# Differential attention by pairs of heads: the products with the values alternate between the halves of the result

## The chip, the core and the metric

The kernel runs on one core of a Trainium2 chip. A core has TensorE (PE in the profile; PEld is its weight load), VectorE (DVE), ScalarE (ACT), GpSimd (POOL) and SyncE (SP), which take their own lists of instructions in order and wait for each other by semaphores, and 16 DMA engines. TensorE writes into PSUM, a small memory of 8 banks of 512 fp32 columns. The metric is the device time of one execution in microseconds; lower is better. The time before is 1351.88 us, the median of three runs (1351.8 to 1352.84).

## What is computed

One decoder layer over 1024 tokens of width 1024: RMSNorm, one wide input projection, three token mixers side by side (Mamba-2 SSD, differential attention, mLSTM), an output projection, a SwiGLU FFN, a gated per-layer input and a last RMSNorm. The change is in the differential attention. It has 4 heads of value width 64; each head makes two softmaxes and subtracts one from the other:

```python
def diff_attention(q, k, v, lam, lam_init, rel_bias, norm_w):
    ...
    for j in range(s_ // Q_BLOCK):
        ...
        sc = jnp.einsum('bqhmd,bkhmd->bhmqk', qb, kb).astype(jnp.float32) * scale
        ...
        sc = sc + jnp.transpose(bias, (2, 0, 1))[None, :, None].astype(jnp.float32)
        sc = jnp.where(dist >= 0, sc, -1e30)
        a = jax.nn.softmax(sc, axis=-1)
        attn = a[:, :, 0] - lam * a[:, :, 1]
        outs.append(jnp.einsum('bhqk,bkhe->bqhe', attn.astype(v.dtype), vb))
    o = jnp.concatenate(outs, axis=1)
    ...
```

## The kernel before

Tokens are on the free axis, features on partitions. The input projection is a stream of matmuls `pj` (in fp32 split into a high and a low part, three matmuls for one) that runs all through the attention: `fill(us)` lets that stream issue as much as `us` microseconds of TensorE's time by an estimate, in steps of three matmuls, and is called after every part of a head. Behind a finished half of a projection ScalarE copies it out (`cst`, `conv`), and VectorE does three steps of a short convolution on it (`conv<-cst`, L594).

The attention goes over two pairs of heads (`hp`), and in each over the eight blocks of 128 queries (`qb`), from the longest to the shortest in the first pair and back up in the second. For one block and one head (`head`, L647) the work is, for each of the two softmaxes `m`: score matmuls into a PSUM bank `sc`, a VectorE operation that adds the bias and takes the minimum (L675, `e<-sc,tb`, one per 512 keys), an exponential on ScalarE with its sum (L678). Then VectorE takes a reciprocal (`rr`, L686), scales it (L687) and combines the two (`e<-e,rr`, L688). TensorE transposes the result by blocks of 128 keys into PSUM (`tp`, L695), up to four blocks at a time, ScalarE copies them to SBUF (`aT`, L698), and TensorE multiplies them with the values (`pv`, L704): weights are 128x64 values of this head, 128 columns are moved, and the result is one half of the partitions of `pv`, the lower for the first head of the pair and the upper for the second. Each fp32 matmul of `pv` is two rows of the profile.

The order on TensorE is the order of the program (class `InOrder`, L84, makes every matmul follow the one before). `run_attention` (L710) sets it: step `u` takes head `u` through its transposes and products, and beside it makes the scores of head `u + 2`, of `u + 3` where the next heads are short (`AHEAD`, L568). The other engines are ordered by the scheduler, by priority: the convolution steps have a low one (`late(L1)`), the copies `aT` a high one.

Of the kernel before, what the change touches and what calls it, by code (L numbers as in the profile page):

```python
# [11 lines left out]
F32 = mybir.dt.float32  # L12
# [7 lines left out]
P = 128  # L20
S = 1024
D = 1024
NT = S // P
# [81 lines left out]
def trunk(ctx: ExitStack, tc: tile.TileContext, a, out):  # L105
    nc = tc.nc
    sync, act, dve, pool, pe = nc.sync, nc.scalar, nc.vector, nc.gpsimd, InOrder(tc, nc.tensor)
# [10 lines left out]
    def right(name, bufs=1):  # L118
        return tc.alloc_tile_pool(name=name, bufs=bufs, side="right", reuse_waits="tile")
# [4 lines left out]
    def psum(name, bufs):  # L124
        return tc.alloc_tile_pool(name=name, bufs=bufs, space=PSUM, reuse_waits="tile")


    ident = const.tile([P, P], F32, name="ident")
# [49 lines left out]
    zp = right("zp", 1)  # L178
    p1pre = right("p1pre", 1)
    dv = p1pre.tile([P, NT, 256], F32, name="dv")  # L180
# [57 lines left out]
    @contextmanager  # L238
    def late(n):

        tc.cur_priority += n
        yield
        tc.cur_priority -= n
# [124 lines left out]
    for t0 in (0, 256):  # L368
        c = slice(t0, t0 + 256)
# [32 lines left out]
    p1 = right("p1", 1)  # L402
    SCB = 3
    psa = psum("psa", 2)
# [37 lines left out]
    def fill(us):  # L442

        owed[0] += us
        while owed[0] > 0 and done[0] < len(jobs):
            step()
# [118 lines left out]


    LATE = 600
    AHEAD = 3  # L568
    AW = 5
    L1, L2, L3 = 200, 0, -100  # L570
    R, F = (34, 42), (2.5, 0.8, 8.0)
# [25 lines left out]
    ym = [ymp.tile([P, 4, H2], F32, tag="ym", name=f"ym{i}") for i in range(2)]  # L597
# [5 lines left out]
    def attention(hp):  # L603

        tb = p1.tile([P, 1280], F32, tag="tb", name="tb", bufs=2)
        pool.memset(tb[:, 256:1024], 0.0)
        for hl, o in ((0, 1024), (1, 0)):  # L610
            sync.dma_start(tb[:, o:o + 256], skew[2 * hp + hl, 127:127 + P * 383]
                           .rearrange("(p u) -> p u", u=383)[:, 0:256])
            pool.affine_select(tb[:, o + P:o + 256], tb[:, o + P:o + 256], pattern=[[-1, P]],
                               compare_op=ALU.is_ge, fill=1e30, base=0, channel_multiplier=1)
        ks = {}

        def load_keys(i):
            ks[i] = p1.tile([P, 4, H2], F32R, tag="ks", name="ks", bufs=2)
            pool.dma_start(ks[i], k_d[hp][:, :, i * H2:(i + 1) * H2])

        for qb in (range(NT - 1, -1, -1) if hp == 0 else range(NT)):
            kl = (qb + 1) * P
            for i in ((0, 1) if qb >= 4 else (0,)):
                if i not in ks:
                    load_keys(i)
            q_ = p1.tile([P, 4, P], F32R, tag="qs", name="qs", bufs=2)
            pool.dma_start(q_, q_d[hp][:, :, qb * P:(qb + 1) * P])

            def col(hl, b, qb=qb):

                return b if hl == 0 or qb == 0 else (b - (qb - 1)) % (qb + 1)

            def runs(hl):

                o = []
                for b in range(qb + 1):
                    if o and col(hl, b) == o[-1][2] + o[-1][1] and col(hl, b) % 4 and b % 4:
                        o[-1][1] += 1
                    else:
                        o.append([b, 1, col(hl, b)])  # L640
                return o

            pv = [None]
            for hl in range(2):
                yield head(hp, qb, hl, q_, ks, tb, col, runs(hl), pv)

    def head(hp, qb, hl, q_, ks, tb, col, runs, pv):  # L647


        kl = (qb + 1) * P  # L650
        ks = dict(ks)
        e = []
        nm = p1.tile([P, 4], F32, tag="nm", name="nm", bufs=6)
        rs0 = asum[:, qb // 4, 4 * (qb % 4) + 2 * hp + hl:4 * (qb % 4) + 2 * hp + hl + 1]
        rs = p1.tile([P, 1], F32, tag="rs", name="rs", bufs=6)
        t_ = tb[:, 1280 - kl:1280] if hl == 0 else tb[:, 0:kl] if qb else tb[:, P:2 * P]
        for m in range(2):
            hm = 2 * hl + m
            if qb >= 4:
                em_ = p1.tile([P, S], F32, tag=f"e{m}", name="e", bufs=3 - m)  # L660
            elif m == 0:
                em_ = p1.tile([P, S], F32, tag=f"e{hl}", name="e", bufs=3 - hl)
            else:
                em_ = e[0][:, H2:]

            low = 3e38
            for c0 in range(0, qb + 1, 4):
                ps = psa.tile([P, H2], F32, tag="sc", name="sc", bufs=SCB)
                for b, n, c in runs:
                    if c // 4 == c0 // 4:  # L670
                        pe.matmul(ps[:, (c - c0) * P:(c - c0 + n) * P], q_[:, hm, :],
                                  ks[b // 4][:, hm, (b % 4) * P:(b % 4 + n) * P], start=True, stop=True)
                cc = slice(c0 * P, min(kl, (c0 + 4) * P))
                acc = nm[:, m + c0 // 2:m + c0 // 2 + 1]
                dve.tensor_tensor_reduce(em_[:, cc], ps[:, 0:cc.stop - cc.start], t_[:, cc], 1.0, low,  # L675
                                         ALU.add, ALU.min, acc)
                low = acc
            last_exp[0] = act.activation(em_[:, 0:kl], em_[:, 0:kl], AF.Exp, bias=low, scale=-1.0,  # L678
                                         accum_out=rs if m else rs0)
            e.append(em_)  # L680
            if m == 0:
                yield
        with late(L2):

            rr_ = p1.tile([P, 1], F32, tag="rr", name="rr", bufs=6)
            dve.reciprocal(rr_, rs)  # L686
            dve.scalar_tensor_tensor(rr_, rs0, rr_, nlam, ALU.mult, ALU.mult)  # L687
            dve.scalar_tensor_tensor(e[0][:, 0:kl], e[1][:, 0:kl], rr_, e[0][:, 0:kl], ALU.mult, ALU.add)  # L688
        yield
        for b0 in range(0, qb + 1, 4):  # L690
            n = min(4, qb + 1 - b0)
            tp = psa.tile([P, 4, P], F32, tag="pt", bufs=6 - SCB, name="tp")
            for b in range(n):
                c = col(hl, b0 + b) * P
                pe.transpose(tp[:, b, :], e[0][:, c:c + P], ident)  # L695
            t_ = zp.tile([P, 4, P], F32, tag="t2", name="aT", bufs=3)
            with late(L3):
                act.copy(t_[:, 0:n, :], tp[:, 0:n, :])  # L698
            yield
            if hl == 0 and b0 == 0:  # L700
                pv[0] = psa.tile([P, P], F32, tag="pt", bufs=6 - SCB, name="pv")
            h = 2 * hp + hl
            for b in range(n):
                pe.matmul(pv[0][hl * 64:(hl + 1) * 64, :], dv[:, b0 + b, h * 64:(h + 1) * 64], t_[:, b, :],  # L704
                          start=(b0 + b == 0), stop=(b0 + b == qb))
        if hl == 1:
            act.copy(ym[qb // 4][:, hp, (qb % 4) * P:(qb % 4 + 1) * P], pv[0])
        yield

    def run_attention():  # L710

        order = [(hp, qb) for hp in range(2) for qb in (range(NT - 1, -1, -1) if hp == 0 else range(NT))
                 for _ in range(2)]
        rate = [R[hp] / (4 * sum(qb + AW for qb in range(NT))) for hp in range(2)]
        src = (head_ for hp in range(2) for head_ in attention(hp))
        heads = []
        for u in range(-2, len(order)):

            small = u >= 0 and all(qb < 4 for _, qb in order[u:u + AHEAD + 1])
            new = []  # L720
            while len(heads) + len(new) <= min(u + (AHEAD if small else 2), len(order) - 1):
                new.append(next(src))
            heads += new
            us = rate[order[u][0]] * (order[u][1] + AW) if u >= 0 else F[0]
            for part in range(2):
                if u >= 0:
                    next(heads[u], None)
                for head_ in new:
                    next(head_)
                fill(us)  # L730
            if u >= 0:
                for _ in heads[u]:
                    pass

    jobs += [conv_job(4 + d, bcg, 4 + d, d) for d in range(4)]
    jobs += [conv_job(8 + d, xg, d, d) for d in range(4)]
    run_attention()
    finish(len(jobs))

# [378 lines left out]
    for half in range(2):  # L1118
# [5 lines left out]
        order = (0, 7, 1, 2, 3, 4, 5, 6)  # L1124
# [251 lines left out]
    for i in (1, 2, 5, 6, 7, 3, 4):  # L1376
        tag = "a" if i in (1, 6, 7, 4) else "b"
# [5 lines left out]
        for k in range(NP):  # L1383
            if k % 4 == 0:
                n = min(4, NP - k)
# [3 lines left out]
            t_ = unit(i, k, bs[:, k % 4], as_ and as_[:, k % 4])  # L1389
# [144 lines left out]
```

## Time and profile before

| what | value |
|---|---|
| median of three runs | 1351.88 us |
| profiled execution, its own time | 1353.48 us |
| its span in the profile | 1351.8 us |
| TensorE busy | 1307.7 us, 97% of the span |
| VectorE / ScalarE / GpSimd busy | 851.9 / 556.9 / 308.7 us |
| chain that ended last, on TensorE | 89% |
| attention: first score matmul to last product | 87 to 262 us |
| granted clock of TensorE, mean of the span / in 87 to 262 us | 0.988 / 1.00 |

Busy is the time in which an engine had an instruction under way; TensorE's overlap, and their ends are modelled, so 97% says only that it is rarely without work. The chain is followed back from the last instruction, at each step to what released it; a share of the chain is what shortening helps. The granted clock is a share of 2.4 GHz.

### The profile page before, as it was taken

What the parts mean: (1) busy time and instruction counts of PE and PEld (TensorE: products, weight loads), DVE (VectorE), ACT (ScalarE), POOL (GpSimd) and SP (SyncE); (2) the same over time, 40 slices, a digit from 0 to 9 for tenths busy, and PEclk for the clock granted to TensorE, in tenths of its full rate; (3) what the DMA queues carried; (4) which work ended last, traced back from release to release, by engine and by line L of the source; (5) the groups of instructions that cost most, each with busy time, mean ns of one, the idle gap of its engine ahead of it and who ended that gap; (6) DMA issues with size and microseconds to landing.
All of it is one profiled execution on the core that took longest, in us unless ns stands there. A gap on an engine that the chain in (4) does not pass through costs nothing.

```text
span 1351.8 us, 17848 instructions
## 1 busy us (share of the span) xinstructions
PE 1307.7 (97%) x6601; PEld 1067.6 (79%) x6601; DVE 851.9 (63%) x1619; ACT 556.9 (41%) x1101; POOL 308.7 (23%) x323
## 2 busy tenths in 40 slices
PE   6999999999999999979999999999979999999997
PEld 5977777777788888758888888888857888888897
DVE  7567778567656855588665564766536796576243
ACT  6346666643323533353333333333323444464121
POOL 4141322243334322242122111222210000000111
PEclk9999999999999999989999999999999999999999
DMA  6472341043312333013332232323389352223011
GB/s 210 164 227 79 80 100 48 19 127 102 91 51 64 104 133 110 32 62 118 117 117 91 96 107 73 114 105 117 120 308 367 112 175 92 80 72 116 8 63 63
DMA packets 66847, 149.84 MB, mean 111 GB/s; under 512 B 6116, under 2 KB 23304, under 8 KB 61640
## 3 DMA queue, kind: packets, MB, share of 16 engines
q1 hardware_dynamic: 52008, 129.82, 28.6%
q0 software_dynamic: 11872, 14.16, 3.9%
q10 hardware_dynamic: 2880, 4.72, 0.9%
q8 instruction: 52, 0.85, 0.3%
q14 instruction: 35, 0.29, 0.1%
HBM read 111.64 MB, written 37.82 MB: 111 GB/s over the span
## 4 chain that ended last, share of the span: by engine, by line
PE 89%; DVE 5%; DMA 3%; ACT 1%; issue 1%; POOL 1%; SPq 0%; POOLq 0%; DVEq 0%; ACTq 0%
PE pd L98 17%; PE a L98 17%; PE pj L98 16%; PE c L98 8%; PE po L98 7%; PE pg L98 6%; PE b L98 4%; PE pv L98 3%; PE pp L98 2%; PE tp L101 1%; PE sc L98 1%; PE py L98 1%; DMA ar<-in_w_down_dram 1%; PE pn L98 1%; PE pk L98 1%
## 5 line engine op out<-in xcount | busy, mean ns | idle before, releaser
L98 PE MATMUL pj<-uT,w 128*128 128x512 f32 x1056 | 276.6, 404 | 0.0
L98 PEld LDWEIGHTS pj<-uT,w 128*128 128x128 f32 x1056 | 192.5, 190 | 36.8 <-issue 0.3
L98 PE MATMUL pd<-un 128*128 128x512 f32 x924 | 212.4, 392 | 5.6 <-DVE un L140 4.7
L98 PEld LDWEIGHTS pd<-un 128*128 128x128 f32 x924 | 174.5, 189 | 43.5 <-DVE un L140 5.1
L140 POOL TENSOR_TENSOR w<-raw,w 128x256 fp32r<-128x256 f32 x88 | 78.6, 921 | 91.8 <-ACT w L139 91.5
L139 ACT CAST un<-ar 128x512 fp32r<-128x512 f32 x77 | 47.9, 622 | 121.4 <-PE pd L98 110.1
L98 PE MATMUL pg<-hT,wg 128*128 128x256 f32 (+1 forms) x576 | 94.0, 319 | 0.0
L98 PE MATMUL po<-yT,wo 128*128 128x512 f32 x384 | 89.8, 395 | 0.0
L98 PEld LDWEIGHTS pg<-hT,wg 128*128 128x128 f32 x576 | 82.7, 188 | 8.5
L98 PEld LDWEIGHTS po<-yT,wo 128*128 128x128 f32 x384 | 71.9, 188 | 16.6
L1500 POOL TENSOR_TENSOR ssq<-ssq,sq 128x256 f32<-128x256 f32 (+1 forms) x18 | 17.1, 952 | 291.2 <-ACT sq L1498 291.2
L140 DVE TENSOR_TENSOR un<-ar,un 128x512 fp32r<-128x512 f32 x77 | 53.0, 688 | 46.7 <-ACT un L139 46.4
L1243 ACT ACTIVATE c<-c 128x512 f32<-128x512 f32 x44 | 27.9, 633 | 98.4 <-DVE c L1242 98.4
L98 PE MATMUL c<-T1h,wX 128*128 128x512 f32 x176 | 59.9, 402 | 3.7 <-ACT wX L139 2.5
L678 ACT ACTIVATE e<-e,nm 128x1024 f32<-128x1024 f32 (+7 forms) x64 | 49.7, 777 | 32.8 <-DVE nm L675 32.5
L98 PE MATMUL a<-T2h,wY 128*128 128x512 f32 x176 | 60.9, 406 | 1.6 <-ACT T2h L139 1.6
L98 PE MATMUL a<-T4h,wV 128*128 128x512 f32 x176 | 60.1, 404 | 2.0 <-DVE c L1246 2.0
L98 PE MATMUL a<-T3h,wZ 128*128 128x512 f32 x176 | 59.1, 397 | 1.1 <-ACT c L1229 1.1
L140 POOL TENSOR_TENSOR wZ<-rgu,wZ 128x512 fp32r<-128x512 f32 x22 | 31.0, 1407 | 122.0 <-ACT wZ L139 110.3
L98 PE MATMUL b<-B21h,wY 128*128 128x512 f32 x176 | 58.6, 394 | 0.0
L98 PE MATMUL c<-B22h,wZ 128*128 128x512 f32 x176 | 58.3, 393 | 0.0
L98 PE MATMUL a<-B11h,wX 128*128 128x512 f32 x176 | 57.9, 390 | 0.0
(385 smaller groups left out, 2667.2 us busy)
## 6 DMA issues: line engine op xcount, KB each, us to landing
rgu<-in_w_gu_dram SPq DMA_DIRECT2D x22, 1024.0 KB, 4.9
opd<-c SPq DMA_DIRECT2D x77, 256.0 KB, 2.0
four<-opd SPq DMA_DIRECT2D x12, 1024.0 KB, 4.9
raw<-in_w_tiles_dram SPq DMA_DIRECT2D x22, 512.0 KB, 3.7
ar<-in_w_down_dram SPq DMA_DIRECT2D x11, 512.0 KB, 9.2
four<-opd SPq DMA_DIRECT2D x6, 768.0 KB, 4.2
xt<-in_x_dram SPq DMA_DIRECT2D x16, 256.0 KB, 4.6
q_d<-qk SPq DMA_DIRECT2D x16, 256.0 KB, 3.5
```

The source lines that it names most:

```text
L98: return self._behind(self.pe.matmul(*args, **kw))
L101: return self._behind(self.pe.transpose(*args, **kw))
L139: act.copy(hi, src)
L140: eng.tensor_tensor(lo, src, hi.bitcast(F32), ALU.subtract)
L678: last_exp[0] = act.activation(em_[:, 0:kl], em_[:, 0:kl], AF.Exp, bias=low, scale=-1.0, accum_out=rs if m else rs0)
L1243: act.activation(g, g, AF.Silu)
L1500: (dve if j == 7 else pool).tensor_tensor(ssq, ssq, sq, ALU.add)
```

## The change

`head` is split. `scores` (one head) ends behind the combination of its two softmaxes. `pair` makes the scores of both heads of a block of queries, and then goes over the keys two blocks at a time: four transposes, alternating between the two heads, into one PSUM tile, one copy `aT` of up to 512 columns, and four products `pv` that alternate between the lower and the upper half of the result. `run_attention` now goes by pairs: step `u` has four parts, and each takes pair `u` one chunk on and makes one part of the scores of pair `u + 1`. The fills of a pair are as many and as long as before. The weights `e` get four buffers for the first softmax and one for the second (three and two before).

```diff
-            pv = [None]
-            for hl in range(2):
-                yield head(hp, qb, hl, q_, ks, tb, col, runs(hl), pv)
+            yield pair(hp, qb, q_, dict(ks), tb, col, [runs(hl) for hl in range(2)])
+
+    def pair(hp, qb, q_, ks, tb, col, runs):
+        es_ = []
+        for hl in range(2):
+            e = []
+            yield from scores(hp, qb, hl, q_, ks, tb, runs[hl], e)
+            es_.append(e[0])
+        pv = None
+        for b0 in range(0, qb + 1, 2):
+            n = min(2, qb + 1 - b0)
+            tp = psa.tile([P, 2, 2, P], F32, tag="pt", bufs=6 - SCB, name="tp")
+            for b in range(n):
+                for hl in range(2):
+                    c = col(hl, b0 + b) * P
+                    pe.transpose(tp[:, b, hl, :], es_[hl][:, c:c + P], ident)
+            t_ = zp.tile([P, 2, 2, P], F32, tag="t2", name="aT", bufs=3)
+            with late(L3):
+                act.copy(t_[:, 0:n], tp[:, 0:n])
+            yield
...
+            for b in range(n):
+                for hl in range(2):
+                    h = 2 * hp + hl
+                    pe.matmul(pv[hl * 64:(hl + 1) * 64, :], dv[:, b0 + b, h * 64:(h + 1) * 64], t_[:, b, hl, :],
+                              start=(b0 + b == 0), stop=(b0 + b == qb))
...
-                em_ = p1.tile([P, S], F32, tag=f"e{m}", name="e", bufs=3 - m)
+                em_ = p1.tile([P, S], F32, tag=f"e{m}", name="e", bufs=4 - 3 * m)
...
-            for b in range(n):
-                pe.matmul(pv[0][hl * 64:(hl + 1) * 64, :], dv[:, b0 + b, h * 64:(h + 1) * 64], t_[:, b, :],
-                          start=(b0 + b == 0), stop=(b0 + b == qb))
...
-        for u in range(-2, len(order)):
-            small = u >= 0 and all(qb < 4 for _, qb in order[u:u + AHEAD + 1])
-            new = []
-            while len(heads) + len(new) <= min(u + (AHEAD if small else 2), len(order) - 1):
-                new.append(next(src))
-            heads += new
+        for u in range(-1, len(order)):
+            new = next(pairs, None)
             us = rate[order[u][0]] * (order[u][1] + AW) if u >= 0 else F[0]
-            for part in range(2):
+            for part in range(4):
                 if u >= 0:
-                    next(heads[u], None)
-                for head_ in new:
-                    next(head_)
+                    next(now, None)
+                if new:
+                    next(new)
                 fill(us)
```

On TensorE, where the first pair's block of 1024 keys ends and that of 896 keys begins, the order before was this. `e_1147` holds the weights of the new block's first head, and the `sc` row at the top is the last of its second head's scores.

```order
L98 MATMUL sc_1249<-ks_996,qs_1136 128x128
L98 MATMUL pj_1164<-uT101_91,w_1075 128x512
L98 MATMUL pj_1164<-uT111_93,w_1075 128x512
L98 MATMUL pj_1164<-uT101_91,w_1075 128x512
L98 MATMUL pj_1268<-uT000_86,w_1099 128x512
L98 MATMUL pj_1268<-uT010_88,w_1099 128x512
L98 MATMUL pj_1268<-uT000_86,w_1099 128x512 [waits Pool_49]
L98 MATMUL pv_1171<-aT_1242,dv_103 64x128 [waits Activation_49]
L98 MATMUL pv_1171<-aT_1242,dv_103 64x128 x3
L101 MATMUL tp_1279<-ident_72,e_1147 128x128 [waits DVE_49]
L101 MATMUL tp_1279<-ident_72,e_1147 128x128 x3
```

After, in the same place; `e_1147` is again the first head's weights and `e_1214` the second's, whose last scores are the `sc` row at the top.

```order
L98 MATMUL sc_1249<-ks_996,qs_1136 128x128
L98 MATMUL pj_1164<-uT101_91,w_1075 128x512
L98 MATMUL pj_1164<-uT111_93,w_1075 128x512
L98 MATMUL pj_1164<-uT101_91,w_1075 128x512
L98 MATMUL pj_1268<-uT000_86,w_1099 128x512
L98 MATMUL pj_1268<-uT010_88,w_1099 128x512
L98 MATMUL pj_1268<-uT000_86,w_1099 128x512 [waits Pool_49]
L98 MATMUL pv_1171<-aT_1242,dv_103 64x128 [waits Activation_49]
L98 MATMUL pv_1171<-aT_1242,dv_103 64x128 x3
L101 MATMUL tp_1279<-ident_72,e_1147 128x128 [waits DVE_49]
L101 MATMUL tp_1279<-ident_72,e_1214 128x128 [waits DVE_49]
L101 MATMUL tp_1279<-ident_72,e_1147 128x128
```

The second transpose now reads the second head's weights, where before four transposes of the first head stood, and those of the second came a head later. On VectorE, at the second head of the block of 256 keys of the second pair (`e_1965` before, reduced from its second scores in the first row):

```order
L675 ISA e_1965,nm_1963<-sc_1975,tb_1849 128x256 [waits PE_49]
L675 ISA nm_1963 128x1
L686 RECIPROCAL rr_1952<-rs_1937 128x1 [waits Activation_49]
L687 SCALAR_TENSOR_TENSOR rr_1952<-asum_983,rr_1952,nlam_802 128x1 [waits DVE_49]
L688 SCALAR_TENSOR_TENSOR e_1938<-e_1938,rr_1952 128x256 [waits DVE_49]
L686 RECIPROCAL rr_1979<-rs_1964 128x1 [waits Activation_49]
L675 ISA e_1994,nm_1992<-sc_1995,tb_1849 128x384 [waits PE_49]
L675 ISA nm_1992 128x1
L687 SCALAR_TENSOR_TENSOR rr_1979<-asum_983,rr_1979,nlam_802 128x1 [waits DVE_49]
L675 ISA e_1994,nm_1992<-sc_2004,tb_1849 128x384 [waits PE_49]
L675 ISA nm_1992 128x1
L688 SCALAR_TENSOR_TENSOR e_1965<-e_1965,rr_1979 128x256 [waits DVE_49]
```

And after, where the same head's weights are `e_1964`:

```order
L698 ISA e_1964,nm_1962<-sc_1972,tb_1865 128x256 [waits PE_49]
L698 ISA nm_1962 128x1
L593 SCALAR_TENSOR_TENSOR conv_1159<-cst_1980,sm_113,conv_1159 128x512 [waits Activation_49,Pool_49]
L709 RECIPROCAL rr_1976<-rs_1963 128x1 [waits Activation_49]
L593 SCALAR_TENSOR_TENSOR conv_1159<-cst_1980,sm_113,conv_1159 128x512 [waits DVE_49]
L710 SCALAR_TENSOR_TENSOR rr_1976<-asum_983,rr_1976,nlam_802 128x1 [waits DVE_49]
L593 SCALAR_TENSOR_TENSOR conv_1159<-cst_1980,sm_113,conv_1159 128x512 [waits DVE_49]
L711 SCALAR_TENSOR_TENSOR e_1964<-e_1964,rr_1976 128x256 [waits DVE_49]
```

The next block's reduces are gone from between this head's reduce and its combination (the last row), and three steps of the convolution have come in.

## Rows read from the trace of the kernel before

**Rows 1.** Chain of waits, 87 to 262 us: shares, then start us, us, what.

```profile
by line: PE pj L98 46.1%; PE pv L98 22.0%; PE tp L101 11.3%; PE sc L98 10.7%; issue 2.8%; DMA k_d<-qk 2.1%; DVE e L675 1.9%; DVE qk L340 0.7%; DVE qk L341 0.6%; ACT e L678 0.5%; ACT aT L698 0.4%; ACT cst L586 0.3%; DVE rr L686 0.1%; DVE nm 
...
106.59 1.02 PE pv L98 x8
...
133.33 0.58 PE pv L98 x4
```

**Rows 2.** Waits of TensorE, 87 to 262 us: who, for whom, us, times, longest.

```profile
PE pv L98 <- ACT aT L698: 0.7, 1, 0.7
```

**Rows 3.** Timeline of TensorE in the SSD stage: start us, us, instruction, count.

```profile
324.35 0.44 PE L98 MATMUL py<-dm,xdt 128*64 128x128 f32 x4
...
325.37 0.70 PE L98 MATMUL pst<-xds,bn 128*128 128x256 f32 x2
```

**Rows 4.** Timeline of all engines, 112 to 115.6 us.

```profile
112.07 0.66 PE L98 MATMUL sc<-ks,qs 128*128 128x256 f32 x4
...
112.56 1.60 PE L98 MATMUL pj<-uT,w 128*128 128x512 f32 x6
112.59 0.69 DVE L675 CUSTOM_DVE_ANT_0 e<-sc,tb 128x512 f32<-128x512 f32 x1 [1.07 <-PE sc L98]
...
113.43 0.62 DVE L675 CUSTOM_DVE_ANT_0 e<-sc,tb,nm 128x384 f32<-128x384 f32 x1
...
114.09 1.04 ACT L678 ACTIVATE e<-e,nm 128x896 f32<-128x896 f32 x1
...
114.10 1.09 PE L98 MATMUL pv<-aT,dv 128*64 128x128 f32 x8
...
115.12 0.66 PE L101 MATMUL tp<-ident,e 128*128 128x128 f32 x4
...
115.53 0.48 PE L98 MATMUL sc<-ks,qs 128*128 128x512 f32 x1
```

**Rows 5.** Groups of VectorE, 87 to 262 us: xcount, busy us, mean ns, idle.

```profile
L688 DVE SCALAR_TENSOR_TENSOR e<-e,rr 128x1024 f32<-128x1024 f32 x4 | 5.7, 1432 | 0.1
...
L688 DVE SCALAR_TENSOR_TENSOR e<-e,rr 128x512 f32<-128x512 f32 x4 | 3.0, 749 | 0.1
...
L688 DVE SCALAR_TENSOR_TENSOR e<-e,rr 128x128 f32<-128x128 f32 x4 | 1.8, 458 | 0.1
```

**Rows 6.** Groups of ScalarE, 87 to 262 us.

```profile
L678 ACT ACTIVATE e<-e,nm 128x512 f32<-128x512 f32 x8 | 5.8, 728 | 3.3 <-DVE nm L675 3.3
...
L678 ACT ACTIVATE e<-e,nm 128x128 f32<-128x128 f32 x8 | 3.2, 402 | 2.2 <-DVE nm L675 2.0
```

**Rows 7.** Timeline at the first pair, second head, 96.8 to 102.6 us.

```profile
96.81 0.63 PE L98 MATMUL sc<-ks,qs 128*128 128x256 f32 x4
...
100.86 1.15 ACT L678 ACTIVATE e<-e,nm 128x1024 f32<-128x1024 f32 x1 [2.33 <-DVE nm L675]
...
102.14 0.16 DVE L686 RECIPROCAL rr<-rs 128x1 f32<-128x1 f32 x1 [1.31 <-ACT e L678]
...
102.60 1.31 DVE L688 SCALAR_TENSOR_TENSOR e<-e,rr 128x1024 f32<-128x1024 f32 x1
```

**Rows 8.** Timeline at the last pair, second head, 243.8 to 249.3 us.

```profile
243.82 0.72 PE L98 MATMUL sc<-ks,qs 128*128 128x256 f32 x4
...
245.91 3.03 DVE L594 SCALAR_TENSOR_TENSOR conv<-cst,sm,conv 128x512 f32<-128x512 f32 x3
...
249.30 1.28 DVE L688 SCALAR_TENSOR_TENSOR e<-e,rr 128x1024 f32<-128x1024 f32 x1
```

**Rows 9.** Timeline of TensorE at two idle stretches; in brackets the idle us.

```profile
276.95 0.33 PE L101 MATMUL pb__2925<-ident,conv 128*128 128x128 f32 x1 [1.97 <-DVE cbm L805]
...
1014.81 1.65 PE L98 MATMUL pd<-un 128*128 128x512 f32 x3 [4.75 <-DVE un L140]
```

**Rows 10.** Windows behind these: us, busy by engine, granted clock, DMA, GB/s.

```profile
277.50:280.90 3.40, 3.40 (x11) 2.17 (x11) 3.40 (x6) 3.40 (x10) 2.21 (x2) 0.50 0.69 226
1011.40:1018.20 6.80, 3.39 (x8) 2.71 (x9) 4.99 (x8) 0.00 (x0) 0.54 (x1) 0.50 1.02 397
```

More of the change, by code (lines that the diff above doesn't have):

```diff
@@ L567, in trunk @@
     LATE = 600
-    AHEAD = 3
     AW = 5
@@ L641, in runs, with scores @@
                 return o
-            pv = [None]
-            for hl in range(2):
-                yield head(hp, qb, hl, q_, ks, tb, col, runs(hl), pv)
-    def head(hp, qb, hl, q_, ks, tb, col, runs, pv):
+            yield pair(hp, qb, q_, dict(ks), tb, col, [runs(hl) for hl in range(2)])
[17 more added lines that the diff above has]
+            yield
+            if b0 == 0:
+                pv = psa.tile([P, P], F32, tag="pt", bufs=6 - SCB, name="pv")
+            for b in range(n):
[3 more added lines that the diff above has]
+                              start=(b0 + b == 0), stop=(b0 + b == qb))
+        act.copy(ym[qb // 4][:, hp, (qb % 4) * P:(qb % 4 + 1) * P], pv)
+    def scores(hp, qb, hl, q_, ks, tb, runs, e):
         kl = (qb + 1) * P
-        ks = dict(ks)
-        e = []
         nm = p1.tile([P, 4], F32, tag="nm", name="nm", bufs=6)
@@ L659, in head @@
             if qb >= 4:
-                em_ = p1.tile([P, S], F32, tag=f"e{m}", name="e", bufs=3 - m)
+                em_ = p1.tile([P, S], F32, tag=f"e{m}", name="e", bufs=4 - 3 * m)
             elif m == 0:
-                em_ = p1.tile([P, S], F32, tag=f"e{hl}", name="e", bufs=3 - hl)
+                em_ = p1.tile([P, S], F32, tag="e0", name="e", bufs=4)
             else:
@@ L689, in head @@
         yield
-        for b0 in range(0, qb + 1, 4):
-            n = min(4, qb + 1 - b0)
-            tp = psa.tile([P, 4, P], F32, tag="pt", bufs=6 - SCB, name="tp")
-            for b in range(n):
[L694 to L703, printed above, removed]
-                pe.matmul(pv[0][hl * 64:(hl + 1) * 64, :], dv[:, b0 + b, h * 64:(h + 1) * 64], t_[:, b, :],
-                          start=(b0 + b == 0), stop=(b0 + b == qb))
@@ L706, in head @@
-        if hl == 1:
-            act.copy(ym[qb // 4][:, hp, (qb % 4) * P:(qb % 4 + 1) * P], pv[0])
-        yield
     def run_attention():
-        order = [(hp, qb) for hp in range(2) for qb in (range(NT - 1, -1, -1) if hp == 0 else range(NT))
-                 for _ in range(2)]
+        order = [(hp, qb) for hp in range(2) for qb in (range(NT - 1, -1, -1) if hp == 0 else range(NT))]
         rate = [R[hp] / (4 * sum(qb + AW for qb in range(NT))) for hp in range(2)]
-        src = (head_ for hp in range(2) for head_ in attention(hp))
@@ L716, in run_attention @@
-        heads = []
-        for u in range(-2, len(order)):
-            small = u >= 0 and all(qb < 4 for _, qb in order[u:u + AHEAD + 1])
-            new = []
-            while len(heads) + len(new) <= min(u + (AHEAD if small else 2), len(order) - 1):
-                new.append(next(src))
-            heads += new
+        pairs = (pair_ for hp in range(2) for pair_ in attention(hp))
+        now = None
+        for u in range(-1, len(order)):
+            new = next(pairs, None)
             us = rate[order[u][0]] * (order[u][1] + AW) if u >= 0 else F[0]
-            for part in range(2):
+            for part in range(4):
@@ L726, in run_attention @@
                 if u >= 0:
-                    next(heads[u], None)
-                for head_ in new:
-                    next(head_)
+                    next(now, None)
+                if new:
+                    next(new)
                 fill(us)
             if u >= 0:
-                for _ in heads[u]:
+                for _ in now:
                     pass
+            now = new
     jobs += [conv_job(4 + d, bcg, 4 + d, d) for d in range(4)]
```

## The prediction

> **What bounds the kernel now.** I began with the chain of waits, cut to the attention (from the first score matmul at 87 us to the last product at 262 us), because the change touches nothing else. The reader is to see that the chain there runs on TensorE: four of its names hold 90% of 175 us, and the products with the values, `pv`, alone 22.0%, 38.5 us [rows 1]. Then the waits of TensorE in the same stretch: there is one, of 0.7 us [rows 2]. So ScalarE and VectorE are always done before TensorE needs them, and a microsecond less on TensorE is a microsecond of the kernel as long as that stays true. Last the timeline of two places: how closely `pv` is issued, and how far ahead of its transposes a head's weights are finished. The second decides.
>
> **What the change saves.** In the chain eight `pv` rows take 1.02 us and four take 0.58 [rows 1]: 0.11 us a row and 0.14 a group. (One fp32 matmul is two rows, so 144 matmuls are 288 rows.) All rows of a group now go to one half of the result. After, four matmuls alternate between the halves. The trace has this pattern elsewhere: `py` of the SSD stage, of the same 128x64 weights and 128 columns, alternates between the halves, and its 16 rows (four entries of four, of which the first is shown) take from 324.35 to 325.37, where the next name begins: again 1.02 us [rows 3]. Less the same 0.14, that is 0.055 us a row. Groups fall from 48 (one for four blocks of a head) to 40 (one for two blocks of a pair). So `pv` falls from 38.5 to 40 x 0.14 + 288 x 0.055 = 21.5 us: **17 us less**. From below: nothing, if here the halves don't overlap. I take 17, since `py` is the same shape.
>
> The same recast saves 8 of 48 copies of `aT` on ScalarE, which the path doesn't see; 8 fewer changes from `pv` to transposes are under 1 us. Four buffers for the first weights and one for the second cost nothing: VectorE's own order puts the combination that reads the second ahead of the reduce that overwrites it. GpSimd's loads of `qs` are still issued while the pair before is at work. The projection matmuls are the same in number between every two score groups.
>
> **What the change adds: a wait at each pair.** Before, a head's scores are made two heads ahead (three, for short ones), so between its second score group and its first transpose stand the whole of another head and three fills. Now a pair's second head has its second score group in the fourth part of the step before, and the very next part opens with transposes of both heads in turn; the second one reads the second head's weights. In the order of TensorE printed with the change only six projections and one `pv` group lie between. TensorE runs its list in order, so projections, scores and products behind the transpose wait too, then their readers.
>
> What must pass meanwhile, for the pair of 896 keys, from the start of the score group [rows 4]: 0.52 us to the first reduce, 0.84 to the second, 0.66 to the exponential, 1.04 for it; then 0.13 to the reciprocal (from 100.86 + 1.15 to 102.14), 0.46 from there to the combination [rows 7], 1.2 for the combination (between the first two of [rows 5]), and, as an estimate, 0.1 to the transpose: 4.9 us. With 1024 keys it is 5.4. For the shorter ones I go down along [rows 5, 6] (one reduce instead of two at 512 and under): 4.5, 4.1, 3.4, 2.95, 2.7, 2.2. Each length comes twice: 60.3 us.
>
> What covers it: the score group itself, about 0.4 (112.07 to 112.56), projections at 1.54 / 6 = 0.26, of which I take 0.235 for those that don't stand ahead of a wait for ScalarE's copy, `pv` at the new price, and the first transpose, a quarter of 0.41 [rows 4]. From the new order I count, over the 16 pairs, 93 projections (3 to 12 each; 21.9 us), `pv` at three of them (1.3), 16 score groups (5.9), 16 transposes (1.6): 30.7 us. So the waits are at least 60.3 - 30.7 = **30 us**, 1 to 3 each, 2.4 at the pair shown.
>
> That supposes VectorE and ScalarE free. At six pairs they aren't. At the first pair, the trace of before shows the very chain: score group at 96.81, combination finished at 102.60 + 1.31 = 103.9, as two operations for the keys of the next heads stand in between [rows 7]; 7.1 instead of 5.4, so 1.7 more. At the last, three convolution steps of 3.03 us stand ahead of the reciprocal and the combination ends at 249.30 + 1.28 = 250.6, 6.8 after 243.82 [rows 8]: 1.4 more. In the new order VectorE keeps these. At the second head of the 128-key pair of the first half and of the 256-key pair of the second, the new order sets convolution steps between reciprocal and combination (printed with the change); at 1.0 each [rows 8], partly beside the exponential: 2.6 more each. Two others 0.8 and 0.2. Together **9 us**. Bounds: from nothing (ScalarE and VectorE come early) to 15, since backlog can also hit pairs that I counted as free.
>
> **What the waits do to the clock.** After 1.97 us without work TensorE ran 277.50 to 280.90 at a granted clock of 0.50, the lower of its levels of 1.2 and 2.4 GHz; after 4.75 us it was 0.50 from 1011.40 to 1018.20 [rows 9, 10]. I find five idle stretches of about 2 us or more in the trace; the low clock came during or behind every one. The low clock for 3.4 us of full work costs 1.7. Eleven of the sixteen waits come out at 2 us or more, so the price lies between nothing and 11 x 1.7 = 19 us. Half of that, **9 us**: some stretches will fall into the next wait, which then only shrinks. The Trainium skill ("TensorE: Matmul & The Clock Gate", section "HAM oscillation") warns of long idle gaps of TensorE; gaps as short as most here would not count by it, and the time would be that of my first rival. The first row of [rows 9] speaks against that reading.
>
> **The sum.** -17 + 30 + 9 + 9 = **+31 us**. The profiled execution took 1353.5 us (span 1351.8, 1.7 around it); the median of the runs shown is 1351.9, so I set the difference on that: **1383 us**. Outside the attention nothing changes but the phase of loads, worth a microsecond or two.
>
> **Rivals.**
> 1. The clock holds. The waits are what I say, and short ones leave 2.4 GHz granted. 1351.9 - 17 + 39 = 1374. For it: the one wait of 0.7 us [rows 2] left the clock of the attention at 1.00 (the table above). Against it: all five stretches.
> 2. The waits are mostly covered and the change is **faster**. The place is the pair's first transposes. If a chain were half as long (30 us) with 31 of cover, nearly no wait is left and 1335 to 1345 comes out; it breaks even where the waits come to 17 us in all, 1.05 per pair. For it: VectorE and ScalarE have idle time in the attention. Against it: the chain is of dependent work at durations that are read from rows, and idle engines shorten none of it.
> 3. The halves don't overlap here: `pv` keeps its 38.5 us, and with waits and clock it is 1400. The new order fixes that matmuls alternate, so only the hardware could deny it; `py` speaks against it.
>
> **Chances.** The forecast with waits and a partly low clock has 0.65 (1375 to 1400), the first rival 0.22 (1363 to 1375), the faster case 0.07, the third 0.06. The range of 1362 to 1400 reaches from the first rival with a few waits less to a low clock behind each wait. A measurement of this kernel tells about 0.2%, 2.7 us, from no change. Within it only the faster case's upper edge falls: 0.03. Faster by more 0.06, slower by more 0.91.
>
> **What the new profile would show.** Eight `pv` rows in 0.58 us, and `pv` near 21 us of the chain. Some 16 waits of TensorE's `tp` on VectorE's combination, 30 to 45 us in total, 2 to 4 us at long pairs, around 1 at the shortest. The granted clock at 0.50 in several stretches of the attention. The same TensorE time in `pj`, `sc` and `tp` otherwise. I am wrong if those waits total less than 17 us, or if `pv` is still 0.11 us a row.

## The result: 3.4% slower, 16 us above the forecast

| | us |
|---|---|
| before, median of 4 runs | 1352.33 (1351.8 to 1352.84) |
| after, median of 4 runs | 1399.02 (1395.24 to 1406.04) |
| ratio | 1.0344, 95% interval 1.0314 to 1.0374 |
| forecast | 1383, range 1362 to 1400 |
| profiled execution of after: its time / its span | 1401.3 / 1399.5 |
| TensorE busy / mean granted clock of the span | 1309.1 us, 94% / 0.973 |

Nearly the whole difference lies in the attention. It ran from 87.0 to 261.5 us before and runs from 88.6 to 308.6 after; behind it 1090 us follow in both.

The chain of waits of the changed kernel, 87 to 309 us (shares by engine and line, then start us, us, what), answers to [rows 1]:

```profile
by line: PE pj L98 27.9%; DVE e L698 9.8%; PE tp L101 8.9%; DVE conv L593 8.8%; DVE e L711 8.1%; issue 7.8%; PE pv L98 7.3%; PE sc L98 6.8%; ACT e L701 5.0%; DVE rr L710 2.2%; ACT conv L590 1.9%; ACT cst L585 1.7%; DVE rr L709 1.4%; DVE qk 
...
109.80 1.05 PE pv L98 x8
...
113.51 0.59 PE pv L98 x8
```

`pv` has fallen from 22.0% of 175 us, 38.5, to 7.3% of 222, 16. Not every group is on this chain: `pv` is busy 26.5 us in all. Eight rows take 0.59 us where 1.02 stood, and 1.05 where the clock is low. VectorE's and ScalarE's operations (reduces L698, combinations L711, convolution L593, exponentials L701 and smaller ones) have grown from some 5% of the chain to some 40%. Not all of that is wait: beside some of these steps TensorE was at work.

What TensorE waits for in that stretch (who, for whom, us in total, times, longest), against the one wait of 0.7 us in [rows 2]:

```profile
PE tp L101 <- DVE e L711: 41.8, 18, 4.9
```

There is no other wait of TensorE. The pair of 896 keys, whose timeline before is [rows 4], in the changed kernel (start us, us, engine, instruction, count, idle before):

```profile
118.16 0.66 PE L98 MATMUL sc<-ks,qs 128*128 128x256 f32 x4
...
118.68 0.69 DVE L698 CUSTOM_DVE_ANT_0 e<-sc,tb 128x512 f32<-128x512 f32 x1 [1.19 <-PE sc L98]
...
119.53 0.62 DVE L698 CUSTOM_DVE_ANT_0 e<-sc,tb,nm 128x384 f32<-128x384 f32 x1
...
120.18 0.66 PE L98 MATMUL pv<-aT,dv 128*64 128x128 f32 x8
120.25 1.04 ACT L701 ACTIVATE e<-e,nm 128x896 f32<-128x896 f32 x1
...
120.77 0.33 PE L101 MATMUL tp<-ident,e 128*128 128x128 f32 x1
...
121.42 0.16 DVE L709 RECIPROCAL rr<-rs 128x1 f32<-128x1 f32 x1 [1.26 <-ACT e L701]
...
121.87 1.15 DVE L711 SCALAR_TENSOR_TENSOR e<-e,rr 128x896 f32<-128x896 f32 x1
...
123.08 0.55 PE L101 MATMUL tp<-ident,e 128*128 128x128 f32 x3 [1.98 <-DVE e L711]
```

The score group begins at 118.16. The last reduce, the exponential, the reciprocal and the combination follow, as forecast, and the second transpose starts at 123.08: 4.9 us later, which is the forecast's number. TensorE had six projections, eight rows of `pv` and one transpose to do, and then nothing for 1.98 us (forecast 2.4).

The stretches of the attention at the lower clock (us, busy us by engine, PEclk as a share of 2.4 GHz, DMA share, GB/s), and among them one at full clock:

```profile
104.60:111.40 6.80, 5.81 (x22) 4.36 (x23) 4.22 (x8) 0.90 (x2) 1.08 (x2) 0.50 0.48 161
148.90:152.30 3.40, 3.36 (x10) 2.68 (x10) 3.36 (x5) 1.57 (x4) 3.40 (x4) 0.50 0.84 215
162.60:166.00 3.40, 3.40 (x13) 2.36 (x13) 2.17 (x5) 1.29 (x3) 0.10 (x1) 0.50 0.01 2
183.10:186.50 3.40, 3.12 (x15) 2.30 (x15) 0.52 (x3) 0.98 (x3) 0.00 (x0) 0.50 0.23 94
193.30:200.10 6.80, 6.76 (x21) 4.91 (x22) 1.85 (x11) 2.52 (x10) 0.47 (x1) 0.50 0.39 122
210.40:217.20 6.80, 6.28 (x23) 4.82 (x24) 1.96 (x6) 2.27 (x6) 0.19 (x1) 0.50 0.27 80
244.50:247.90 3.40, 3.40 (x10) 2.83 (x11) 1.19 (x4) 1.31 (x2) 0.00 (x0) 0.50 0.00 0
247.90:275.20 27.30, 21.04 (x135) 15.56 (x134) 19.06 (x47) 15.53 (x33) 6.14 (x8) 1.00 0.12 29
275.20:278.60 3.40, 3.40 (x11) 2.72 (x10) 3.06 (x7) 0.85 (x2) 0.10 (x1) 0.50 0.00 0
292.30:299.10 6.80, 4.98 (x16) 3.65 (x18) 1.78 (x5) 4.32 (x4) 0.73 (x1) 0.50 0.01 2
```

Nine stretches, 44.2 us in all, with 40.5 us of TensorE's work in them: at half speed that work costs 20 us, as an estimate; experiment 4 tests it. The forecast had 9.

### The profile page after: what moved, and what is told of

Same layout as the page of the kernel before. It is cut to its first block, busy times and chain, and to the rows that moved or that the text cites. A ratio compares the mean times of both kernels' runs of the same rounds, so it can differ in the third digit from the quotient of the medians.

```text
span 1399.5 us, 17826 instructions
## 1 busy us (share of the span) xinstructions
PE 1309.1 (94%) x6601; PEld 1063.9 (76%) x6601; DVE 859.6 (61%) x1619; ACT 556.9 (40%) x1093; POOL 310.8 (22%) x323
## 4 chain that ended last, share of the span: by engine, by line
PE 80%; DVE 11%; DMA 3%; ACT 3%; issue 2%; POOL 1%; SPq 0%; DVEq 0%; POOLq 0%; ACTq 0%
PE pd L98 17%; PE a L98 15%; PE pj L98 14%; PE c L98 7%; PE po L98 6%; PE pg L98 6%; PE b L98 3%; DVE e L698 2%; PE pp L98 2%; PE tp L101 1%; DVE conv L593 1%; DVE e L711 1%; PE pv L98 1%; PE sc L98 1%; PE py L98 1%
## 5 line engine op out<-in xcount | busy, mean ns | idle before, releaser
L98 PE MATMUL pj<-uT,w 128*128 128x512 f32 x1056 | 285.1, 414 | 0.0
L98 PEld LDWEIGHTS pj<-uT,w 128*128 128x128 f32 x1056 | 199.3, 197 | 38.6 <-issue 0.2
L101 PE MATMUL tp<-ident,e 128*128 128x128 f32 x144 | 30.0, 313 | 41.8 <-DVE e L711 41.8
L701 ACT ACTIVATE e<-e,nm 128x1024 f32<-128x1024 f32 (+7 forms) x64 | 49.7, 777 | 47.0 <-DVE nm L698 44.9
L698 DVE CUSTOM_DVE_ANT_0 e<-sc,tb 128x512 f32<-128x512 f32 (+3 forms) x64 | 37.6, 588 | 46.2 <-PE sc L98 45.5
```

What stands on the lines that cost most here:

```text
L98: return self._behind(self.pe.matmul(*args, **kw))
L101: return self._behind(self.pe.transpose(*args, **kw))
```

## The experiments

**1. The four products of a group: two of the first head, then two of the second.**

```diff
-            for b in range(n):
-                for hl in range(2):
+            for hl in range(2):
+                for b in range(n):
```

> Only the order of the four products of a group is changed: both blocks of the first head, then both of the second, so that the rows no longer alternate between the halves. Theory (-17 for the alternation, the rest of the change is waits and clock): eight rows of pv take 0.9 to 1.02 us instead of 0.59, pv is busy 12 to 16 us more, the waits of the transposes stay at about 41 us, and the time is 12 to 16 us above that of the changed kernel (1399): 1411 to 1415. Rival (the halves are not what made pv shorter; it is the wider group of both heads): pv stays at 0.59 and the time at 1395 to 1404.

Measured: 1398.55 us (ratio to before 1.0334, 1.0307 to 1.0361), the same as the changed kernel. The chain of this kernel at the place of the row at 113.51 above:

```profile
114.31 0.59 PE pv L98 x8
```

Still 0.59 us. The expectation failed and the rival's number came. So strict alternation isn't what shortens the group. Either the halves work beside one another all the same, or something else in the form by pairs does it.

**2. The same form, one half.** From a pair's third block on, the second head's products go to the lower half too.

```diff
-                    pe.matmul(pv[hl * 64:(hl + 1) * 64, :], dv[:, b0 + b, h * 64:(h + 1) * 64], t_[:, b, hl, :],
...
+                    lo = hl * 64 if b0 == 0 else 0
...
+                    pe.matmul(pv[lo:lo + 64, :], dv[:, b0 + b, h * 64:(h + 1) * 64], t_[:, b, hl, :],
...
```

> As the changed kernel, but from a pair's third block of keys on the products of the second head are added to the lower half as well (so the result of those blocks is not that of the reference). 24 of the 40 groups, 168 of the 288 rows, are then of one half, with both heads' operands and the wide copy as before. Theory (the two halves work beside one another, be the rows alternating or two and two): eight rows of these groups take 1.02 us again, pv is busy 8 to 10 us more, 1404 to 1411 with nearly the same waits. Rival (what made a group shorter is the form by pairs, not the halves): 0.59 stays in all groups and the time is 1395 to 1403.

Measured: 1404.0 us (1398.4 to 1411.6; ratio 1.038, 1.0348 to 1.0413). The same group in the chain:

```profile
112.67 1.02 PE pv L98 x8
```

1.02 us, the price of before, with both heads' operands, the wide copy and the same waits (41.5 us). `pv` is busy 36.0 us instead of 26.5. So it is the halves. The rival of experiment 1 falls with this, though its number had come. The time alone would not have told: it lies in the range of the changed kernel's runs (1395.24 to 1406.04).

The starts of the single rows in the traces show how. In one half, in the kernel before, they stand 0.109 us apart. In the changed kernel two rows start within 0.006 us, and the next two 0.109 us later. So the matmuls of the two halves run at the same time; it is not only that one half's weights are loaded while the other multiplies.

**3. How far apart the two halves may stand.** The products of two groups are issued together: four of the lower half and then four of the upper; and in a second kernel the same 16 rows alternating. 

> As the changed kernel, but the products of two groups are issued together, four of the lower half and then four of the upper (16 rows). Theory A (matmuls of the second half need not be next to one of the first: four may stand ahead): 16 rows in 1.0 to 1.1 us, the same 0.055 a row. Theory B (only neighbours, or neighbours but one, overlap): 16 rows in 1.3 to 1.8 us. The time of the kernel is 1392 to 1412 either way, as products move a part later.

```diff
+            done = done + [(b0 + b, t_[:, b]) for b in range(n)]
+            if len(done) < 4 and b0 + n <= qb:
+                continue
-            for b in range(n):
-                for hl in range(2):
+            for hl in range(2):
+                for i, t in done:
```

> As the run with products of two groups issued together, but the 16 rows alternate between the halves matmul by matmul again. That run took 1.51 us for 16 rows as four of the lower half and then four of the upper. Theory (the order decides: only matmuls that stand close overlap): 16 rows in 1.0 to 1.1 us, about 3 to 5 us less in all. Rival (a group of 16 rows is slower for its length): 1.5 us again.

The first in the chain, then the second:

```profile
112.05 1.51 PE pv L98 x16
```

```profile
110.16 1.02 PE pv L98 x16
```

1.51 us for 16 rows in blocks of four matmuls, 1.02 alternating. At 0.11 a row and 0.14 a group, 16 rows of one half would be 1.90, and eight 1.02. Both 16 rows in blocks of four and 8 rows in blocks of two are about 0.4 us shorter than that: as an estimate, four rows' worth, two matmuls, run beside the other half, and no more. The starts of the 16 rows in blocks of four agree: the first four and the last four stand 0.11 us apart (0.16 behind the very first), the eight between them, from 112.47 to 112.85, half as far. That is why two and two cost the same as alternation, and four and four don't. The times are single runs: 1393.86 and 1392.44. The second came out 1.4 less, not the 3 to 5 expected, but in its attention 44.2 us ran at 0.50 against 27.2 in the first, so the two times can't show what the groups are worth.

The Trainium skill ("TensorE: Matmul & The Clock Gate", section "Part 3: Packing small matmuls — row/col tiling") has matmuls start and end strictly in order. By that, two and two would overlap only where the halves meet, and experiment 1 would have been slower. The 0.59 us disagrees.

**4. The price of the clock.** Ten matmuls of 512 columns, whose result nobody reads, ahead of each pair's first transposes.

```diff
+            if b0 == 0:
+                for _ in range(FILLER):   # 10
+                    pe.matmul(tp[:, 0:n], uh(0, 0)[:, 0:P], uh(0, 1)[:, 0:n * 256], start=True, stop=True)
```

> Ahead of each pair's first transposes ten projection-sized matmuls (512 columns, 0.26 us each) write into the PSUM tile that the transposes then overwrite; their result is used by nothing. They add work of about 2.6 us at each of 16 places, 42 us in all, and keep TensorE busy in the wait. By the waits of the changed kernel (1.0 to 4.9 us each) about 8 us of wait are left and 8 us of the filler lie beyond it. Theory (the idle stretches bring the low clock, and it costs about 21 us): the clock stays at 1.00 nearly throughout the attention, and the time falls to 1381 to 1392 in spite of the work added. Rival A (the low clock has another cause, or costs next to nothing): 1404 to 1410, with stretches of 0.50 left. Rival B (the forecast's 9 us for the clock was right, and the waits are longer than they look): 1395 to 1400.

Measured: 1387.15 us (1384.57 to 1388.91; ratio 1.0239, 1.0212 to 1.0266): 12 us less than the changed kernel, with more work. One filler in the timeline, TensorE's wait for the combinations, and the window of the attention:

```profile
118.68 2.60 PE L98 MATMUL tp<-uT 128*128 128x512 f32 x10
```

```profile
PE tp L101 <- DVE e L715: 12.4, 10, 2.6
```

```profile
88.00:301.00 213.00, 199.84 (x1148) 152.87 (x1147) 135.21 (x343) 115.72 (x258) 45.18 (x63) 0.98 0.23 60
```

The fillers keep TensorE busy for 37 us (34.6 at 14 pairs, 2.7 at the two shortest), and the waits are 29 us less. That alone would be 8 us more. The clock is what pays: a mean of 0.98 in the attention, two stretches of 3.4 us at 0.50 where 44.2 us were. This separates the clock from the waits: 12 + 8 = 20 us for 37 us of low clock, about half.

**5. One and two parts later.** A pair's transposes and products are taken from the scores by another part, or two, of the step.

```diff
+        LAG = 1                 # second kernel: 2
...
+        for g in range(4 * len(order) + 4 + LAG):
+            u, part = g // 4 - 1, g % 4
+            if part == 0:
+                made.append(next(pairs, None))
+            v = (g - LAG) // 4 - 1
...
+            if v >= 0:
+                next(made[v], None)
+            if made[g // 4]:
+                next(made[g // 4])
+            fill(us)
```

> Each pair's transposes and products start one part later (a quarter of a step), so one score group more, one fill more and a group of products of the pair before stand between a pair's last score group and its first transposes; everything else as in the changed kernel. Theory (the loss is the wait for the chain from score group to combination, and the clock behind it): a part is about 2.5 us on average, so of 41 us of wait 5 to 12 are left, with one to three stretches at 0.50; -17 + 8 + 3 on 1352 is 1346, range 1338 to 1354. Rival (the loss is in the form of the work by pairs: groups of two blocks, buffers four and one): at least 1385. Rival (the low clock comes without idle stretches): stretches of 0.50 remain as many as before and the time is 1360 to 1370.

> As the run before, but two parts later, about the distance that the kernel before kept between a head's scores and its transposes. The four buffers of the weights now are read later, so the first score reduce of the pair after next can wait for a transpose of a long pair. Theory: waits of the transposes under 3 us in all, no stretch at 0.50, 1335 to 1340, unless the buffers bring waits of another kind (score reduces waiting for transposes, then TensorE for the score banks): then 1340 to 1350. Rival (form of the work by pairs): at least 1380. Rival (alternating halves save nothing when waits are gone): 1350 to 1354.

Measured: 1362.5 us (ratio 1.0071, 1.0048 to 1.0094) and 1347.45 (0.9952, 0.9935 to 0.9968). Waits of TensorE and the window of the attention, one part later:

```profile
PE tp L101 <- DVE e L711: 19.1, 14, 3.3
PE pv L98 <- ACT aT L662: 0.4, 1, 0.4
```

```profile
88.00:275.00 187.00, 167.21 (x979) 124.43 (x979) 131.06 (x342) 114.23 (x255) 45.49 (x63) 0.96 0.27 68
```

And two parts later:

```profile
PE tp L101 <- DVE e L711: 4.6, 4, 2.2
PE sc L98 <- DVE nm L698: 3.2, 4, 1.6
PE pv L98 <- ACT aT L662: 1.4, 3, 0.7
```

```profile
88.00:259.00 171.00, 162.36 (x970) 122.13 (x968) 130.28 (x343) 113.00 (x255) 43.52 (x63) 0.98 0.29 75
```

Both miss what was expected of the waits: 19 us are left one part later instead of 5 to 12, and two parts later the transposes wait 4.6 us instead of under 3, and 9.2 with the other two lines. The first time lies above its range and falls into a rival's band (1360 to 1370), but that rival wanted as many low stretches as before, and there are three, 13.6 us of 44. The second lies in the band that was given for late buffers (1340 to 1350), but in its trace no reduce of VectorE waits for a transpose. No rival of form holds: with the same groups and buffers the loss is gone. What keeps some waits is VectorE's list. At the longest one that is left, two parts later (VectorE's steps and TensorE's transposes):

```profile
166.73 2.61 DVE L593 SCALAR_TENSOR_TENSOR conv<-cst,sm,conv 128x512 f32<-128x512 f32 x1
...
170.01 0.48 DVE L711 SCALAR_TENSOR_TENSOR e<-e,rr 128x256 f32<-128x256 f32 x1
...
170.54 0.90 PE L101 MATMUL tp<-ident,e 128*128 128x128 f32 x3 [2.22 <-DVE e L711]
```

One step of the convolution took 2.61 us, to 169.34, and the combination that the transpose waits for came behind it.

**6. The backlog of VectorE.** The changed kernel without the three convolution steps.

```diff
-            with late(L1):
-                for i in range(3):
-                    dve.scalar_tensor_tensor(o, st[:, i:i + H2], cw[:, j, i:i + 1], o, ALU.mult, ALU.add)
```

> As the changed kernel, without VectorE's three convolution steps on the halves of eight projections during the attention (this part of the result is left out). Theory (the forecast's term of 9 us: backlog of VectorE lengthens the chain at some pairs): the waits of the transposes fall from 41.8 to 30 to 34 us, and the time by 9 to 15 with the low clock behind them, to 1384 to 1390. Rival (the steps only fill VectorE's idle time): waits 39 to 42, time 1394 to 1402.

Measured: 1380.81 us (ratio 1.0208, 1.0181 to 1.0234), 18 us less, more than expected. TensorE's wait and its window:

```profile
PE tp L101 <- DVE e L708: 32.0, 16, 3.7
```

```profile
87.00:293.00 206.00, 173.43 (x971) 128.63 (x971) 99.08 (x306) 115.09 (x254) 41.09 (x66) 0.93 0.26 67
```

The waits fall from 41.8 to 32.0. The forecast's 30, and 1.7 for the first pair whose backlog is not convolution, make 31.7. Of the rest of the 18 some 7 are clock (30.6 us at 0.50 instead of 44.2, a mean of 0.93 instead of 0.90); the last 2 lie within the spread of the runs.

**7. Both together.** Two parts later, and the convolution steps held back until the pair's second combination has been issued, or at the latest until the next half of a projection is copied out.

```diff
         def evac(ps, half):
+            flush()                   # issues what is held
...
-            with late(L1):
-                for i in range(3):
-                    dve.scalar_tensor_tensor(o, st[:, i:i + H2], cw[:, j, i:i + 1], o, ALU.mult, ALU.add)
+            def steps():
...                                   # the same three, behind the last combination on VectorE
+            held.append(steps)
...
+            last = dve.scalar_tensor_tensor(e[0][:, 0:kl], e[1][:, 0:kl], rr_, e[0][:, 0:kl], ALU.mult, ALU.add)
...
+        if hl:
+            flush()
```

> The version two parts later, and the convolution steps of VectorE issued behind the combination of the pair's second head instead of where they come ready. Theory (in the version two parts later the waits left, 4.6 us of transposes, 3.2 of score groups, 1.4 of products, come from convolution steps in VectorE's order): they halve, the stretch at 0.50 behind the longest one goes, and the time is 1338 to 1344. Rival (the steps held back keep ScalarE's copies of the projections waiting, and with them TensorE): 1347 or more.

Measured: **1339.69 us** (1337.09 to 1341.43; ratio to before 0.9899, 0.9880 to 0.9917). Waits and window:

```profile
PE sc L98 <- DVE nm L710: 2.1, 3, 1.4
PE tp L101 <- DVE e L723: 1.4, 2, 0.9
PE pv L98 <- ACT aT L674: 1.3, 3, 0.7
```

```profile
87.00:251.00 164.00, 159.06 (x974) 119.65 (x972) 129.13 (x343) 113.70 (x259) 42.01 (x64) 1.00 0.30 77
```

The waits halve, as expected: 4.8 us instead of 9.2, nearly all of it at the transposes, which wait 1.4 us instead of 4.6. The clock is 1.00 all through. This version beats both kernels, the one before by 1.0%.

To see whether the held steps alone would do it, the kernel before got the same edit. 

> The kernel before, by heads, with only the convolution steps of VectorE moved behind the combination of a pair's second head, as in the version that took 1339.7 us. Theory (the kernel before has no wait that the steps could lengthen, so the 13 us of that version are the alternation and its waits): 1350 to 1355. Rival (a good part of those 13 us is worth having without pairs): 1341 to 1349.

Measured: 1355.01 us (ratio 1.001, 1.0001 to 1.002). Nothing is gained without the pairs, as the first theory had it.

Last, the version of 1339.69 us with the alternating edit of experiment 3. 

> The version two parts later with the convolution steps held back (1339.7 us), and in it the products of two groups issued together, alternating (16 rows in 1.02 us, as the run of that edit alone showed). Groups fall from 40 to 24; at 0.14 us each that is 2.2 us. Theory (a group's fixed 0.14 is saved where nothing waits): 1335 to 1339. Rival (the products of a pair now end later, and buffers of aT or of the weights that come free later bring new waits): 1340 to 1345.

Measured: 1339.16 us (0.9902, 0.9885 to 0.9920): no difference. TensorE's waits in it:

```profile
PE sc L98 <- DVE nm L714: 4.2, 3, 2.2
PE tp L101 <- DVE e L727: 3.0, 4, 1.1
PE pv L98 <- ACT aT L674: 0.2, 1, 0.2
```

The 2 us of the groups are there (`pv` is busy 22.1 us instead of 24.6), and the score groups wait 2 us more for VectorE's reduces, the transposes 1.6 more, with one low stretch again. The rival's waits came and cancelled the gain, but not for its reason: ahead of the longest one (2.2 us) VectorE was not waiting for a buffer. It ran a combination and two of the held convolution steps (2.37 us from 114.45) before the reduce that frees the score bank.

## Why the prediction was right, and the term that was mis-sized

- **The saving, -17: right.** `pv` is busy 41.7 us before and 24.6 in the version at full clock (experiment 7). (On the chain of the changed kernel, where the forecast looked for 21 us, stand 16, as part of the groups is off it.) Its reason was a little too narrow: the halves overlap up to two matmuls apart, not only alternating (experiments 1 to 3).
- **The waits, +30, and the backlog, +9: right in sum.** 39 were forecast and 41.1 more than before measured. The parts hold apart as well: 32.0 without the convolution against 31.7, 9.8 from it against 7.3. By pair the backlog is coarser, and that its sum came so near is partly luck: 2.9 and 1.5 us at the two pairs with a forecast of 2.6, 1.7 at the last (1.4), and 2.0 and 1.3 at two pairs (256 keys in the first half, 640 in the second) that were given 0.8 at most. So the longest waits stand at short pairs too, where the forecast had 2 to 4 us at long ones and around 1 at the shortest. The pair of 256 keys in the second half, forecast with 2.6 of backlog, shows it (VectorE's list, then TensorE's first transposes):

```profile
206.16 0.75 DVE L593 SCALAR_TENSOR_TENSOR conv<-cst,sm,conv 128x512 f32<-128x512 f32 x1 [0.76 <-ACT conv L590]
...
206.83 0.15 DVE L709 RECIPROCAL rr<-rs 128x1 f32<-128x1 f32 x1
...
206.95 1.24 DVE L593 SCALAR_TENSOR_TENSOR conv<-cst,sm,conv 128x512 f32<-128x512 f32 x1
208.12 0.67 DVE L710 SCALAR_TENSOR_TENSOR rr<-asum,rr,nlam 128x1 f32<-128x1 f32 x1
208.71 1.29 DVE L593 SCALAR_TENSOR_TENSOR conv<-cst,sm,conv 128x512 f32<-128x512 f32 x1
209.93 0.94 DVE L711 SCALAR_TENSOR_TENSOR e<-e,rr 128x256 f32<-128x256 f32 x1
...
210.92 0.90 PE L101 MATMUL tp<-ident,e 128*128 128x128 f32 x3 [4.86 <-DVE e L711]
```

  Three convolution steps stand ahead of the combination, two of them behind the reciprocal. TensorE waits 4.86 us, the longest of all; in the run without the steps the wait there was 1.95, so they cost 2.9.
- **The clock, +9: the mis-sized term.** It measured 20, above its own bound of 19. Of the 16 us that the time lies above the forecast the clock makes 11 and the waits 2; 1.6 more lie ahead of the attention, which begins that much later. The range held by 1 us. Two sentences of the step failed. The bound took one stretch of 3.4 us for each of eleven waits, but four of nine stretches lasted 6.8 us. And half was struck off because low stretches would fall into the next wait; of 44.2 us only 3.7 were idle, since mostly 7 to 15 us lie between two waits, more than these stretches lasted.
- **The rivals.** The first (the clock holds, 1374) is out by experiment 4, the covered case by the waits, the third by 0.59 us. The Trainium skill ("TensorE: Matmul & The Clock Gate", section "HAM oscillation") warns of longer gaps than most of these. The windows above disagree: 0.50 came behind waits of 2.07 and 2.57 us as well (from 148.9 and 162.6).

The account closes. From the span of before, 1351.8, less 17.1 for `pv` and 0.7 for the wait that goes, plus the waits of TensorE and half of the low stretches in the attention:

| kernel | waits | low stretches | worked out | measured span |
|---|---|---|---|---|
| after | 41.8 | 44.2 | 1397.9 | 1399.5 |
| fillers (37.3 us of them added) | 13.1 | 6.8 | 1387.8 | 1387.2 |
| one part later | 19.5 | 13.6 | 1360.3 | 1360.6 |
| two parts later | 9.2 | 6.8 | 1346.6 | 1346.9 |
| without convolution steps | 32.6 | 30.6 | 1381.9 | 1379.2 |
| two parts later, steps held back | 4.8 | 0 | 1338.8 | 1338.7 |

Six kernels, none off by more than 2.7 us, with a range of 60. By the same sum the kernel of experiment 1 comes to 1398.0 (span 1397.1) and the last one, with its own `pv` of 22.1, to 1340.6 (1339.2). The three of experiments 2 and 3, with `pv` priced by their rows, are further off: 1403.4 for 1409.8, 1387.3 for 1391.6, 1395.1 for 1390.7. So the account is good to some 6 us. Why the low clock lasts 3.4 us behind one wait and 6.8 behind another was not settled.

## What to carry to other kernels

A change that shortens TensorE's work but brings a consumer close behind its producer is priced by that distance: the dependent chain through the other engines, less what TensorE has to do meanwhile, at every place. Here 41 us of such waits, and 20 of clock behind them, stood against 17 of saving. The cure was to keep the saving, restore the distance and take side work out of the chain's way. Waits of TensorE cost more than their length: add what the clock takes behind them, here half of the waits again.

## What was not expected of the hardware

- Products of the two halves overlap also two and two: eight rows in 0.59 us, as when they alternate; four and four don't (1.51 us for 16 rows against 1.02).
- The lower clock came with waits of some 2 us, like the shorter one of [rows 9], but the wait's own length doesn't decide alone. In the changed kernel these two transposes (idle in brackets) differ:

```profile
148.94 0.90 PE L101 MATMUL tp<-ident,e 128*128 128x128 f32 x3 [2.07 <-DVE e L711]
```

```profile
259.38 0.55 PE L101 MATMUL tp<-ident,e 128*128 128x128 f32 x3 [3.04 <-DVE e L711]
```

  Behind 2.07 us the clock was 0.50 from 148.9; behind 3.04 us it stayed at 1.00 until 275.2, as the windows above show. In the version with held steps the longest wait was 1.4 us and the attention stayed at 1.00; two parts later it was 0.50 from 108.8, behind waits of 1.53 and 0.49 us. The trace of before even has a stretch at 0.50 without any wait of TensorE, in it or in the 16 us ahead of it, which the forecast, starting from the idle stretches, passed over. Shortly ahead of it stand 16 matmul rows of two columns each:

```profile
379.84 1.84 PE L98 MATMUL ms<-sel,sq 128*128 128x2 f32 x16
```

```profile
383.30:386.70 3.40, 3.40 (x10) 2.72 (x9) 1.19 (x4) 0.00 (x0) 2.61 (x2) 0.50 0.00 0
```

  What else decides, no run here shows.
- The runs of the changed kernel spread over 11 us and follow the mean granted clock of the span: it was 0.976 at 1395.24 us and 0.971 at 1406.04.
